# Sums of weight and activation blocks in DRAM, given out group by group instead of in one run, and the additions to the merged blocks put ahead of the last addition to T4

## The chip, the cores and the metric

The kernel runs on one core of a Trainium2 chip. The metric is the device time of one execution in microseconds (us). TensorE (PE) multiplies, VectorE (DVE) and ScalarE (ACT) work on tiles in SBUF, GpSimd (POOL) and SyncE (SP) here mostly issue DMAs. Each engine works through its own queue in order, and waits on semaphores that other engines and DMAs raise.

## The reference, cut to what matters

One layer with a sequence of 1024 and a width of 1024, in float32:

```
h = x @ w_in + b_in            # six blocks of 1024 columns: xa, za, xb, zb, ga, gb
ya = RG_LRU(causal_conv4(xa)) * silu(za)
yb = multi_scale_pool(xb) * silu(zb)
merged = sigmoid(ga) * (ya @ w_proj_a) + sigmoid(gb) * (yb @ w_proj_b)
y = merged @ w_out + b_out
out = layer_norm(2 ** 0.25 * x + y)
```

The two products `ya @ w_proj_a` and `yb @ w_proj_b` are the ones whose operands this change is about.

## The kernel before

Each 1024 x 1024 product is cut into 2 x 2 blocks of 512 and done by Strassen's scheme as Winograd wrote it: seven products of blocks instead of eight, whose operands are sums and differences of blocks. Each product of float32 numbers is three matmuls of a high and a low part (`passes`).

**First stage (to about 530 us).** `x @ w_in` is done in 24 groups of seven products, listed in `order`: first G0, A0, G1, A1 and so on to G7 and A7, then B0 to B7. An A group gives a block of 128 columns of xa and za, a B group of xb and zb, a G group of the gates. A group takes products m1, m7, then what `between()` brings from the groups before (the product m3 of the last group, the gate matmuls `ps_g` of an older A group, the pooling matmuls of an older B group), then m6, m2, m4, m5. ACT copies m1, m7 and m6 out of PSUM (`copied`, line 166; `t7` is the copy of m7). The weights of the next group are loaded by SP into the tiles `ra` and `rb` (lines 109 and 110), split by ACT into high parts (line 85) and by DVE into low parts (line 86), and summed on DVE (lines 124 to 129). Tiles for weights are 14, so SP issues a load only when an older tile is free. The order on PE is written by hand; on ACT and DVE a scheduler sets it, and SP issues in the order of the program.

**Sums in DRAM.** The second stage needs for each of the two products seven operands from the weights (`p1` to `p4` are their sums) and seven from the activations (`t1` to `t4`, from the blocks `ya` and `yb` that the first stage stores). These sums are made by DMA alone: `summed` issues on POOL's queue a plain copy of 1 MB from DRAM to DRAM and then additions (`add_to`, a DMA that adds to its destination, 1 MB too). `weight_sums` has 8 such DMAs for each product (16 in all), `input_sums1` has 5, `input_sums2` has 4. Before the change all are issued where they are called: `input_sums1("a")` and the 16 weight sums stand one behind the other in POOL's queue when the fourth A block's `ya` is stored, at about 228 us, and `input_sums2("b")` with four additions stands in the second stage, where the last blocks of `yb` are stored.

**Second stage, the merge (about 533 to 703 us).** The 14 products of `steps` (a: 1, 2, 6, 5, 3, 7, 4; b: 1, 2, 6, 7, 5, 4, 3) run one after the other on PE, four tiles each (`g`). The raw operands of a step are loaded two steps ahead (`load`), cast one step ahead (`cast`), and SP, ACT and DVE do their parts in the order written. For b the merged block `sums` gets its second term by an addition DMA (`add_to(of(sums, d, h), u)`, the rows `m<-m_b` and `m<-um_b`), and one step later `split_m` on ACT (line 852) and DVE (line 853) splits it, which waits for that DMA. In the loop over `g` a step does `cast(i + 1, g)`, then one `split_m` of the step before, then the copies out of PSUM. `xb4r` is the raw operand T4 of step (b, 4), loaded from `t4b`; `wor` are raw blocks of `w_out` (`load_wo`, `cast_wo`).

**Third stage (703 to 799 us).** `merged @ w_out` (`ps_o`) and the layer norm.

Of the kernel before, what the change touches and what calls it, by code (L numbers as in the profile page):

```python
# [7 lines left out]
F32 = mybir.dt.float32  # L8
# [4 lines left out]
P = 128  # L13
# [3 lines left out]
H = 512  # L17
# [24 lines left out]
def layer_kernel(ctx: ExitStack, tc: tile.TileContext, xq, x, w_in, par, wg, w_pool, wpa, wpb, w_out, rows, out):  # L42
    nc = tc.nc
# [5 lines left out]
    const = pool("const", 1)  # L49
# [231 lines left out]
        nc.sync.dma_start(y_d[n][c], y)  # L281


    def summed(name, *terms):
        t = dram.tile([KQ, P, H], F32, tag=name, name=name)
        nc.gpsimd.dma_start(t, terms[0])
        for u in terms[1:]:
            add_to(t, u)
        return t

    def add_to(t, u):
        nc.gpsimd.dma_start(t, u, accum_op=ALU.add, max_dma_last_dim=2048)

    def weight_sums(n, w):
        a11, a12, a21, a22 = (w[KQ * i:KQ * i + KQ, :, KQ * k:KQ * k + KQ, :].rearrange("n p k m -> n p (k m)")
                              for i in range(2) for k in range(2))
        p1 = summed(f"p1{n}", a21, a22)
        p2 = summed(f"p2{n}", a11, p1)
        src["w", n] = {1: a11, 2: a12, 4: a22, 5: p1, 6: p2, 7: summed(f"p3{n}", a11, a21),
                       3: summed(f"p4{n}", a12, p2)}  # L300


    def input_sums1(n):
# [3 lines left out]

    def input_sums2(n):
        b21, b22 = (y_d[n][KQ:, :, sl] for sl in HALF)
        for j in (6, 7, 4):  # L310
            add_to(src["x", n][j], b22)
        add_to(src["x", n][4], b21)
        src["x", n].update({2: b21, 3: b22})

    src = {}
# [35 lines left out]
    def a_gates(c, xc, xh, xl, sz):  # L351
        gh, gl = gw[c]
        if c + 1 < NK:
            load_g(c + 1)

        r, i = kt(f"r{c}"), kt(f"i{c}")
        for h in range(2):
            pg = [bank(f"ps_g{c}_{h}_{n}") for n in range(2)]
            for k, (w, m) in enumerate(((gh, xh), (gh, xl), (gl, xh))):
                for n in range(2):  # L360
                    nc.tensor.matmul(pg[n], w[HEAD[n], :], m[HEAD[n], HALF[h]], start=k == 0, stop=k == 2)  # L361
            for t, half, ps, s, cb in ((r, LO, pg[0], LO, C_BR), (r, HI, pg[1], HI, C_BR),
                                       (i, LO, pg[0], HI, C_BI), (i, HI, pg[1], LO, C_BI)):
                A.activation(t[half, HALF[h]], ps[s], AF.Sigmoid, bias=par_sb[s, cb + c:cb + c + 1])  # L364

        a = kt(f"a{c}")
        A.activation(a, r, AF.Exp, scale=sc_a[:, c:c + 1])  # L367
        t = r
        A.activation(t, r, AF.Tanh, scale=sc_t[:, c:c + 1])
        V.tensor_tensor(i, i, xc, ALU.mult)  # L370
        V.scalar_tensor_tensor(i, a, 1.0, i, ALU.add, ALU.mult)  # L371
        V.scalar_tensor_tensor(a, a, 1.0, t, ALU.add, ALU.mult)
        V.tensor_scalar(a, a, -1.0, 1.0, ALU.mult, ALU.add)
        A.activation(t, t, AF.Sqrt)
        V.tensor_tensor(i, i, t, ALU.mult)
        hs = t
        V.tensor_tensor_scan(hs, a, i, 0.0, ALU.mult, ALU.add)  # L377
        V.tensor_tensor(hs, hs, sz, ALU.mult)
        A.mul(hs[:, negative(c)], hs[:, negative(c)], -1.0)
        store_y("a", c, hs)  # L380
        if c == KQ - 1:
            input_sums1("a")
            weight_sums("a", wpa)
            weight_sums("b", wpb)
        elif c == NK - 1:
            input_sums2("a")

# [339 lines left out]

    prev_m3 = prev_end = None
    due, last, ends, W = {}, [], [], {}
    for i in range(1, len(order)):  # L730
        kind, c = order[i]
        if i + 1 < len(order):
            W[i + 1] = load_group(i + 1)
        if kind == "B" and c % 2 == 1:
            load_wp(c // 2)
        if i == 1:
            tiles = tiles0
        elif kind == "A":
            tiles, takes = a_outputs(c)
        elif kind == "B":  # L740
            tiles, takes = b_outputs(c)
        else:
            finish, takes = g_outputs(GA if c < 4 else GB, c % 4)
        if i > 1:
            g = Group(f"{kind}{c}", W.pop(i), X, *takes)

        def between():
            for f in due.pop(i, []):
                f()
            if prev_m3:  # L750
                prev_m3()
            if prev_end:
                prev_end()

        if i == 1:
            prev_m3 = None
        elif i >= len(order) - 2:
            g.sums(between)
            prev_m3 = None
            last.append(g)  # L760
        else:
            g.m1()
            g.m7()
            between()
            g.m6()
            g.m2()
            g.m4()
            g.m5()
            if kind == "B" and order[i - 1][0] == "A":
                for f in due.pop(i + 1, []):  # L770
                    f()
            prev_m3 = g.m3
        if kind == "A":
            def prev_end(c=c, tiles=tiles, i=i):
                front = a_front(c, *tiles)
                due.setdefault(i + 2, []).append(lambda: a_gates(c, *front, tiles[1]))
        elif kind == "B":
            def prev_end(c=c, tiles=tiles, i=i):
                for _ in b_front(c, *tiles):
                    pass  # L780
                if c % 2 == 1:
                    due.setdefault(i + 2, []).append(lambda: b_pool(c // 2))
        else:
            prev_end = finish
        if i >= len(order) - 2:
            ends.append((c, *tiles))
            prev_end = None
# [74 lines left out]
    def cast_wo(e, k, raw):  # L862
        hl = wt(f"wo{e}_{k}") if e == 0 else xt(f"wo{e}_{k}")
        split(raw, hl[:, 0, :], hl[:, 1, :])
        wo[e, k] = (hl[:, 0, :], hl[:, 1, :])

    load(0)
    load(1)
    parts6 = [getattr(g, f) for f in ("rest1", "m2", "rest3") for g in last]
# [14 lines left out]
    for i, (n, j) in enumerate(steps):  # L884
        load_sg(i + 1)
        load(i + 2)
        if (n, j) == ("a", 7):
            b_pool(3)
            input_sums2("b")
        if j == 1:  # L890
            a, c, m1, um = [[None] * KQ for _ in range(4)]
        X_, W_ = ([(hi_[:, k, :], lo_[:, k, :]) for hi_, lo_ in ops[i][o:o + 2] for k in range(2)] for o in (0, 2))
        for g in range(KQ):
            if j == 1:
                a[g] = bank(f"pa_{n}{g}")
            elif j == 7:
                c[g] = bank(f"pc_{n}{g}")
            ps = a[g] if j in (1, 6, 5, 3) else c[g] if j != 2 else bank(f"pe_{n}{g}")
            for q in range(KQ):
                sl = slice(q * P, (q + 1) * P)  # L900
                passes(ps, (W_[g][0][:, sl], W_[g][1][:, sl]), X_[q],
                       j in (1, 2, 7) and q == 0, j in (2, 4, 3) and q == KQ - 1)
            cast(i + 1, g)
            if now:
                now.pop(0)()
            if i >= 2:
                next(pieces, None)
            if j == 1:
                m1[g] = et(f"m1_{n}{g}")
                A.copy(m1[g], ps)  # L910
            elif j in KEEP[n]:
                if j == 6:
                    um[g] = wt(f"um_{n}{g}", F32, (P, S)) if n == "a" else kt(f"um_{n}{g}")
                A.copy(um[g][:, HALF[KEEP[n][j]]], ps)
            if (n, j) in DONE:
                d, h = DONE[n, j]
                d += g
                if j == 3:
                    t, u = ps, et(f"c12_{n}{g}") if n == "b" else None
                else:  # L920
                    t = u = m1[g] if j == 2 else um[g][:, HALF[h]]
                    V.tensor_tensor(t, ps, t, ALU.add)
                if n == "a":
                    if d % 2 == 0:
                        sums[d // 2, h] = xt(f"m{d}{h}", F32)
                    V.tensor_tensor(of(sums, d, h), t, sgs[i][g], ALU.mult)
                else:
                    V.tensor_tensor(u, t, sgs[i][g], ALU.mult)
                    if j == 3:
                        V.tensor_tensor(of(sums, d, h), of(sums, d, h), u, ALU.add)  # L930
                        split_m(j, d, h)
                    else:
                        add_to(of(sums, d, h), u)
                        later.append(lambda j=j, d=d, h=h: split_m(j, d, h))
            k = KQ * (i - 9) + g
            if 2 <= k < NK + 2:
                cast_wo(0, k - 2, raws_wo.pop(0))
            if 0 <= k < NK:
                raws_wo.append(load_wo(0, k))
        now, later = later, []  # L940
    merge.close()


# [114 lines left out]
```

## Time and profile before

| | |
|---|---|
| runs | 800.3, 800.05, 797.32 us; median 800.05 |
| profiled execution | 800.89 us, of which the span of the trace is 799.1 |
| PE busy | 759.8 us, 95% of the span |
| DVE, ACT, POOL busy | 74%, 53%, 5% of the span |
| mean granted PE clock | 0.976 of full speed |
| DMA | 139 MB; POOL's queue 38.8 MB, 22.6% of the 16 DMA engines' time |

Busy time is that of an engine between the start and the end of its instructions; a wait shows as idle time ahead of an instruction, with what ended it. The chain of waits is followed back from the last instruction, at each step to what released it. The granted clock is a share of 2.4 GHz: 0.50 is 1.2 GHz. A DMA's row gives its issue; its landing is read from the chain, from the wait that it ended, or from the median of its group.

### The profile page before, as it was taken

What the parts mean: (1) busy time and instruction counts of PE and PEld (TensorE: products, weight loads), DVE (VectorE), ACT (ScalarE), POOL (GpSimd) and SP (SyncE); (2) the same over time, 40 slices, a digit from 0 to 9 for tenths busy, and PEclk for the clock granted to TensorE, in tenths of its full rate; (3) what the DMA queues carried; (4) which work ended last, traced back from release to release, by engine and by line L of the source; (5) the groups of instructions that cost most, each with busy time, mean ns of one, the idle gap of its engine ahead of it and who ended that gap; (6) DMA issues with size and microseconds to landing.
All of it is one profiled execution on the core that took longest, in us unless ns stands there. A gap on an engine that the chain in (4) does not pass through costs nothing.

```text
span 799.1 us, 8834 instructions
## 1 busy us (share of the span) xinstructions
PE 759.8 (95%) x3308; PEld 616.9 (77%) x3308; DVE 589.9 (74%) x764; ACT 423.5 (53%) x543; POOL 40.0 (5%) x67
## 2 busy tenths in 40 slices
PE   8979999999999999896899998999999959999996
PEld 6857788878888888685688887788888848888885
DVE  5997695959586968593967766467988727967587
ACT  5575859595958584956734354234652436430000
POOL 0000000000010100100001001000000020300000
PEclk9999999999999999997999999999999989999999
DMA  8042222222259988795287338568669999656022
GB/s 316 13 161 73 86 82 106 83 106 83 106 155 331 228 218 252 200 221 150 83 167 184 95 121 261 184 222 308 237 227 274 239 263 370 143 146 258 20 87 106
DMA packets 56587, 139.06 MB, mean 174 GB/s; under 512 B 4256, under 2 KB 7456, under 8 KB 56480
## 3 DMA queue, kind: packets, MB, share of 16 engines
q1 hardware_dynamic: 41920, 99.69, 35.0%
q0 software_dynamic: 14624, 38.80, 22.6%
q8 instruction: 26, 0.43, 0.2%
q14 instruction: 17, 0.14, 0.0%
HBM read 114.36 MB, written 56.62 MB: 214 GB/s over the span
## 4 chain that ended last, share of the span: by engine, by line
PE 57%; DVE 18%; issue 9%; ACT 8%; DMA 7%; SPq 1%; POOL 0%; DVEq 0%; ACTq 0%; POOLq 0%
PE ps_o L968 11%; PE a_B L91 7%; PE pa_a L91 5%; PE a_G L91 5%; PE a_A L91 4%; PE pc_b L91 3%; PE c_G L91 3%; PE pa_b L91 3%; PE ps_pool L91 3%; PE c_B L91 2%; PE c_A L91 2%; PE e_B L91 2%; DMA rb_B<-in_w_in 2%; ACT i L364 2%; DVE r L377 1%
## 5 line engine op out<-in xcount | busy, mean ns | idle before, releaser
L968 PE MATMUL ps_o<-wo,m 128*128 128x512 f32 (+1 forms) x408 | 88.5, 379 | 0.0
L968 PEld LDWEIGHTS ps_o<-wo,m 128*128 128x128 f32 x408 | 73.5, 188 | 15.0
L345 DVE SCALAR_TENSOR_TENSOR xc<-xp,par_sb,xc 128x1024 f32<-128x1024 f32 x24 | 30.7, 1281 | 0.3
L852 ACT ACTIVATE m<-m 128x512 fp32r<-128x512 f32 x16 | 9.8, 629 | 39.4 <-DMA m<-m_b 21.0
L125 DVE TENSOR_TENSOR p_G<-p_G,ra_G 128x512 f32<-128x512 f32 x7 | 4.8, 692 | 28.9 <-PE a_G L91 28.9
L91 PE MATMUL pa_a<-oh,oh 128*128 128x512 f32 x64 | 24.9, 389 | 0.0
L91 PE MATMUL pa_a<-ol,oh 128*128 128x512 f32 x64 | 24.9, 389 | 0.0
L91 PE MATMUL pa_a<-oh,ol 128*128 128x512 f32 x64 | 24.9, 389 | 0.0
L91 PE MATMUL pa_b<-oh,oh 128*128 128x512 f32 x64 | 24.9, 389 | 0.0
L91 PE MATMUL pa_b<-ol,oh 128*128 128x512 f32 x64 | 24.9, 389 | 0.0
L91 PE MATMUL pa_b<-oh,ol 128*128 128x512 f32 x64 | 24.9, 389 | 0.0
L364 ACT ACTIVATE r<-ps_g,par_sb 64x512 f32<-64x512 f32 x32 | 21.9, 684 | 3.9 <-PE ps_g L361 3.4
L853 DVE SCALAR_TENSOR_TENSOR m<-m,m 128x512 fp32r<-128x512 f32 x16 | 10.8, 687 | 16.5 <-ACT m L852 16.5
L91 PE MATMUL c_A<-x64h,wd_A 128*128 128x512 f32 x64 | 21.4, 393 | 1.0 <-ACT x64h L594 1.0
L508 DVE SCALAR_TENSOR_TENSOR zb<-ps_pool,par_sb,zb 128x512 f32<-128x512 f32 x16 | 12.0, 749 | 14.0 <-PE ps_pool L91 14.0
L364 ACT ACTIVATE i<-ps_g,par_sb 64x512 f32<-64x512 f32 x32 | 21.9, 684 | 0.5
L91 PE MATMUL pc_b<-oh,oh 128*128 128x512 f32 x32 | 13.6, 424 | 8.7 <-ACT oh L85 8.7
L972 DVE TENSOR_TENSOR z<-ps_o,z 128x512 f32<-128x512 f32 (+1 forms) x17 | 11.1, 657 | 14.1 <-PE ps_o L968 14.0
L91 PE MATMUL c_B<-x64h,wd_B 128*128 128x512 f32 x64 | 21.0, 389 | 0.0
L980 ACT ACTIVATE sd<-mv,eps 128x1 f32<-128x1 f32 x8 | 2.4, 295 | 34.9 <-DVE mv L979 34.9
L371 DVE SCALAR_TENSOR_TENSOR i<-a,i 128x1024 f32<-128x1024 f32 x8 | 9.8, 1226 | 14.9 <-ACT a L367 14.9
L91 PE MATMUL ps_pool<-mixh,wp 128*128 128x512 f32 x64 | 20.7, 394 | 0.0
(447 smaller groups left out, 2401.8 us busy)
## 6 DMA issues: line engine op xcount, KB each, us to landing
sg<-sg SPq DMA_DIRECT2D x16, 512.0 KB, 2.7
ra_A<-in_w_in SPq DMA_DIRECT2D x8, 512.0 KB, 3.4
rb_A<-in_w_in SPq DMA_DIRECT2D x8, 512.0 KB, 3.8
ya<-r SPq DMA_DIRECT2D x8, 512.0 KB, 2.7
ra_B<-in_w_in SPq DMA_DIRECT2D x8, 512.0 KB, 4.0
rb_B<-in_w_in SPq DMA_DIRECT2D x8, 512.0 KB, 7.1
yb<-zb SPq DMA_DIRECT2D x8, 512.0 KB, 3.0
sgla<-sg SPq DMA_DIRECT2D x8, 512.0 KB, 6.1
```

Of the source, the lines that this page charges most:

```text
L91: nc.tensor.matmul(ps, a, b, start=first and i == 0, stop=last and i == 2, skip_group_check=True)
L125: V.tensor_tensor(self.p23[:, 0, :], self.p14[:, 0, :], ra[:, 0, :], ALU.add)
L345: V.scalar_tensor_tensor(xc, xp[:, j:j + S], pcol(C_CONVW, 4 * c + j), xc, ALU.mult, ALU.add)
L364: A.activation(t[half, HALF[h]], ps[s], AF.Sigmoid, bias=par_sb[s, cb + c:cb + c + 1])
L371: V.scalar_tensor_tensor(i, a, 1.0, i, ALU.add, ALU.mult)
L377: V.tensor_tensor_scan(hs, a, i, 0.0, ALU.mult, ALU.add)
L508: V.scalar_tensor_tensor(y[:, HALF[h]], ps, pcol(C_BP, c), y[:, HALF[h]], ALU.add, ALU.mult)
L852: A.mul(of(mh, d, h), of(sums, d, h), sign)
L853: V.scalar_tensor_tensor(of(ml, d, h), of(sums, d, h), sign, of(mh, d, h).bitcast(F32), ALU.mult, ALU.subtract)
L968: nc.tensor.matmul(ps, l, r, start=(k == 0 and i == 0), stop=(k == NK - 1 and i == 2))
L972: nc.vector.tensor_tensor(zt[s][:, lo:hi], ps, zt[s][:, lo:hi], ALU.add)
L980: nc.scalar.activation(sd, mv[:, 1:2], AF.Sqrt, bias=eps)
```

## The change

The DMAs of the sums are no longer issued where they are called. `summed` and `input_sums2` put them into a list, `jobs`, and `run_jobs` issues the first ones of it: two in each G and B group, one in each A group, from the third group on. Ahead of each portion stands a copy of one column of `t7` by ACT into `pace` and a copy of that by POOL, so that POOL reaches the portion when ACT has copied the group's m7. The weight sums are put on the list ahead of the loop, in another order (`p3` ahead of `p2`). In the merge three of the four DMAs of `input_sums2("b")` are issued where all four were, and the fourth, the second addition to T4, behind step (b, 2), whose four additions to `sums` so come ahead of it.

```diff
+    def run_jobs(n, i=None, t=None):
+        if jobs and i is not None:
+            A.copy(pace[:, i:i + 1], t[:, 0:1])
+            nc.gpsimd.tensor_copy(paced[:, i:i + 1], pace[:, i:i + 1])
+        for _ in range(min(n, len(jobs))):
+            jobs.pop(0)()
...
-        nc.gpsimd.dma_start(t, terms[0])
+        jobs.append(lambda: nc.gpsimd.dma_start(t, terms[0]))
         for u in terms[1:]:
-            add_to(t, u)
+            jobs.append(lambda: add_to(t, u))
...
-        for j in (6, 7, 4):
-            add_to(src["x", n][j], b22)
-        add_to(src["x", n][4], b21)
+        for j, u in ((6, b22), (7, b22), (4, b22), (4, b21)):
+            jobs.append(lambda j=j, u=u: add_to(src["x", n][j], u))
...
             input_sums1("a")
-            weight_sums("a", wpa)
-            weight_sums("b", wpb)
...
+    weight_sums("a", wpa)
+    weight_sums("b", wpb)
     for i in range(1, len(order)):
...
+        if i >= 2:
+            run_jobs(1 if kind == "A" else 2, i, g.t7)
...
+    run_jobs(len(jobs))
     load(0)
...
             input_sums2("b")
+            run_jobs(3)
...
         now, later = later, []
+        if (n, j) == ("b", 2):
+            run_jobs(1)
```

The order of instructions on PE, DVE and SP is the same in both programs. On ACT 19 copies of one column are added, each behind or soon behind the copy of m7 of its group. On POOL, where the sums of the weights stand, the queue before is one run of DMAs (`p1b` and so on are the sums, `in_wpb` the weights):

```order
L292 DMA p4a<-p2a 512x512
L286 DMA p1b<-in_wpb 512x512
L292 DMA p1b<-in_wpb 512x512
L286 DMA p2b<-in_wpb 512x512
L292 DMA p2b<-p1b 512x512
L286 DMA p3b<-in_wpb 512x512
L292 DMA p3b<-in_wpb 512x512
```

Now the same DMAs stand in portions, each behind a copy that waits for ACT. L301 is the plain copy, L297 the addition. The rows are those of the groups A3, G4, A4, G5 and A5:

```order
L301 DMA p1b<-in_wpb 512x512
L292 COPY paced<-pace 128x1
L297 DMA p1b<-in_wpb 512x512
L301 DMA p3b<-in_wpb 512x512
L292 COPY paced<-pace 128x1
L297 DMA p3b<-in_wpb 512x512
L292 COPY paced<-pace 128x1
L301 DMA p2b<-in_wpb 512x512
L297 DMA p2b<-p1b 512x512
L292 COPY paced<-pace 128x1
L301 DMA p4b<-in_wpb 512x512
```

So one run became portions: G groups get an addition with a copy behind it, or a copy with the addition that depends on it, or two copies; A groups get one DMA.

In the merge POOL's queue before has both additions to T4 (`t4b`) ahead of the four additions to the merged blocks (`m`, from `m_b`):

```order
L292 DMA t2b<-yb 512x512
L292 DMA t3b<-yb 512x512
L292 DMA t4b<-yb 512x512 x2
L292 DMA m_4149<-m_b_4726 128x512
L292 DMA m_4149<-m_b_4745 128x512
L292 DMA m_4188<-m_b_4764 128x512
L292 DMA m_4188<-m_b_4783 128x512
```

Now the second addition to T4 stands behind the four:

```order
L297 DMA t3b<-yb 512x512
L297 DMA t4b<-yb 512x512
L297 DMA m_4189<-m_b_4765 128x512
L297 DMA m_4189<-m_b_4784 128x512
L297 DMA m_4228<-m_b_4803 128x512
L297 DMA m_4228<-m_b_4822 128x512
L297 DMA t4b<-yb 512x512
L297 DMA m_4594<-um_b_4941 128x512
```

One 1 MB DMA has moved behind four of 256 KB; what follows is as it was.

## Rows read from the trace of the kernel before

**Rows 1.** Timeline of PE where it waited: start, us, instruction, [idle before <-releaser].

```profile
321.75 0.49 PE L361 MATMUL ps_g<-xch,gh 64*128 64x512 f32 x2 [0.62 <-ACT xch L85]
323.81 0.51 PE L361 MATMUL ps_g<-xcl,gh 64*128 64x512 f32 x2 [1.56 <-DVE xcl L86]
...
364.75 0.80 PE L361 MATMUL ps_g<-xch,gh 64*128 64x512 f32 x2 [5.02 <-ACT xch L85]
367.11 0.79 PE L361 MATMUL ps_g<-xcl,gh 64*128 64x512 f32 x2 [1.56 <-DVE xcl L86]
...
398.20 0.50 PE L91 MATMUL a_B<-x13h,wch_B 128*128 128x512 f32 x1 [2.69 <-DVE xbp L441]
...
656.74 0.80 PE L91 MATMUL pc_b<-oh,oh 128*128 128x512 f32 x1 [8.67 <-ACT oh L85]
```

**Rows 2.** Table of stretches: length, PE, PEld, DVE, ACT, POOL busy, PEclk, DMA.

```profile
324.40:327.70 3.30, 3.30 (x12) 2.35 (x10) 1.16 (x3) 3.30 (x5) 0.00 (x0) 0.50 1.07 186
361.90:372.10 10.20, 5.78 (x18) 3.85 (x19) 4.28 (x6) 6.92 (x9) 1.03 (x1) 0.50 0.61 165
399.40:402.80 3.40, 3.40 (x9) 2.65 (x9) 0.52 (x1) 0.10 (x1) 0.00 (x0) 0.50 0.99 176
652.00:662.20 10.20, 5.43 (x12) 3.84 (x13) 7.93 (x10) 8.94 (x14) 0.57 (x1) 0.50 0.95 250
```

**Rows 3.** Chain of waits, first stage: issue, us to landing, DMA.

```profile
230.31 5.72 DMA ra_G<-in_w_in
...
271.45 4.46 DMA ra_G<-in_w_in
...
311.34 8.29 DMA ra_B<-in_w_in
...
355.29 9.85 DMA rb_B<-in_w_in
```

**Rows 4.** Timeline of SP: three issues of loads.

```profile
190.38 0.33 SPq L109 DMA_DIRECT2D ra_G<-in_w_in  x1
...
354.85 0.34 SPq L109 DMA_DIRECT2D ra_B<-in_w_in  x1
...
661.26 6.21 SPq L859 DMA_DIRECT2D wor<-in_w_out  x4
```

**Rows 5.** The tile ra_G: its seven loads.

```profile
DMA to landing us min/median/max: 3.2/3.5/5.7
```

**Rows 6.** Timeline of POOL: five rows of its DMA issues.

```profile
227.75 1.07 POOL L286 DMA_DIRECT2D t1a<-ya  x1 [226.42 <-DMA ya<-r]
...
305.56 1.04 POOL L286 DMA_DIRECT2D p1b<-in_wpb  x1
...
640.86 1.03 POOL L292 DMA_DIRECT2D t4b<-yb  x1 [13.72 <-DMA t4b<-yb]
641.49 3.05 POOL L292 DMA_DIRECT2D m<-m_b  x3
651.71 0.85 POOL L292 DMA_DIRECT2D m<-m_b  x1 [7.18 <-issue]
```

**Rows 7.** Timeline of ACT: a copy of m7, a split of a merged block, a cast.

```profile
305.69 0.57 ACT L166 COPY m_G<-c_G 128x512 f32<-128x512 f32 x1
...
652.68 0.63 ACT L852 ACTIVATE m<-m 128x512 fp32r<-128x512 f32 x1 [21.02 <-DMA m<-m_b]
...
670.00 0.62 ACT L85 CAST wo<-wor 128x512 fp32r<-128x512 f32 x1 [1.40 <-DMA wor<-in_w_out]
```

**Rows 8.** Timeline of DVE in the merge.

```profile
637.95 0.69 DVE L928 TENSOR_TENSOR m_b<-m_b,sglb 128x512 f32<-128x512 f32 x1
...
671.60 1.23 DVE L86 TENSOR_TENSOR ol<-wb5r,oh 128x1024 fp32r<-128x1024 f32 x1 [0.26 <-ACT oh L85]
...
679.69 1.22 DVE L86 TENSOR_TENSOR ol<-wb4r,oh 128x1024 fp32r<-128x1024 f32 x1
```

**Rows 9.** Chain of waits in the merge: one product on PE.

```profile
670.69 10.88 PE pa_b L91 x48
```

More of the change, by code (lines that the diff above doesn't have):

```diff
@@ L281, in store_y, with add_to @@
         nc.sync.dma_start(y_d[n][c], y)
+    jobs = []
+    pace = const.tile([P, 32], F32, name="pace")
+    paced = const.tile([P, 32], F32, name="paced")
+    def run_jobs(n, i=None, t=None):
[4 more added lines that the diff above has]
+            jobs.pop(0)()
+    def add_to(t, u):
+        nc.gpsimd.dma_start(t, u, accum_op=ALU.add, max_dma_last_dim=2048)
     def summed(name, *terms):
         t = dram.tile([KQ, P, H], F32, tag=name, name=name)
-        nc.gpsimd.dma_start(t, terms[0])
+        jobs.append(lambda: nc.gpsimd.dma_start(t, terms[0]))
         for u in terms[1:]:
-            add_to(t, u)
+            jobs.append(lambda: add_to(t, u))
         return t
-    def add_to(t, u):
-        nc.gpsimd.dma_start(t, u, accum_op=ALU.add, max_dma_last_dim=2048)
     def weight_sums(n, w):
@@ L297, in weight_sums @@
         p1 = summed(f"p1{n}", a21, a22)
+        p3 = summed(f"p3{n}", a11, a21)
         p2 = summed(f"p2{n}", a11, p1)
-        src["w", n] = {1: a11, 2: a12, 4: a22, 5: p1, 6: p2, 7: summed(f"p3{n}", a11, a21),
-                       3: summed(f"p4{n}", a12, p2)}
+        src["w", n] = {1: a11, 2: a12, 4: a22, 5: p1, 6: p2, 7: p3, 3: summed(f"p4{n}", a12, p2)}
     def input_sums1(n):
```

## The prediction

> **What bounds the kernel now.** PE is busy for 95% of the span, so the time can fall only where PE waits or runs at half clock. I read first PE's timeline for idle time ahead of an instruction [rows 1]. The places that this change can reach are four: the gate matmuls at 321.75 (0.62 and 1.56 us), the next ones at 364.75 (5.02 and 1.56), a group of products at 398.20 (2.69) and the merge at 656.74 (8.67). Then I read the granted clock around these places [rows 2]: behind each of them stands a stretch at 0.50 of the clock, which is 1.2 GHz. What PE worked in such a stretch took twice its time, so half of it is lost: 1.65, 2.9, 1.7 and 2.7 us. The three places in the first stage so cost 2.18 + 1.65 + 6.58 + 2.9 + 2.69 + 1.7 = 17.7 us, and the one in the merge 8.67 + 2.7 = 11.4 us.
>
> Third, the chain of waits says why. Through the first stage it goes from the load of a group's weights through ACT and DVE to the next such load [rows 3]. The load issued at 230.31 took 5.72 us and the next was issued 41.14 later; that one took 4.46 and the next came 39.89 later; that one took 8.29 and the next [rows 4] came 43.51 later. Take the load off and 35.42, 35.43 and 35.22 us are left: the pair of groups costs ACT and DVE 35.4 us and a load. PE's own pace for a pair is 39.93 (190.38 to 230.31) [rows 3, 4], where nothing waited. So a load may take 4.5 us; each microsecond above that puts ACT and DVE one later against PE. Loads with nothing beside them take 3.2 to 3.5 us [rows 5]. The load at 230.31 had one copy of the sums beside it, issued at 227.75; the one at 311.34 had an addition and a copy, the latter issued at 305.56 [rows 3, 6]. By 311 the lateness was 1.2, and the load of 8.29 made it 5.0; PE then waited 2.18. It so lets 2.8 us of lateness pass without a wait.
>
> In the merge ACT stands for 21 us at the split of a merged block, line 852, until the addition `m<-m_b` has landed [rows 7]. The casts of the next step's operands stand behind it on ACT, and PE waits for those. The addition was ready to go early: DVE wrote the last of the four blocks to be added at 637.95 + 0.69 [rows 8]. But POOL stood until 640.86 for the first addition to T4 to land, issued the second, and then the `m` additions; these landed behind it [rows 6, 7].
>
> **The change, part by part.**
>
> *Sums in portions, first stage.* The 16 weight sums now begin in G1, at some 66 us, and the sums of `ya` come in G6 to A7. No byte is added; what counts is which loads fall beside a sum. A portion starts when ACT has copied m7, in a G group 305.69 + 0.57 [rows 7], and the load that the chain goes through is issued in the same group, 5 us later (311.34) [rows 3]. So in every G group from G2 on that load meets the portion, where before only the loads from 230 on did. In G2, G4 and G6 the portion is an addition with a copy behind it, as at 311: I take 8.29 us, 3.8 above what PE's pace allows. In G3, G5 and G7 it begins with a copy, as at 230: 5.72, so 1.2. Lateness adds up, PE waits for what is above 2.8, and a wait of 2 us or more brings a half-clock stretch (1.7 us lost, by which ACT and DVE catch up): the shortest wait that I read ahead of one is the 2.18. Group by group:
> G2: 3.8 late, PE waits 1.0, 2.8 stay. G3: 4.0 late, waits 1.2, 2.8 stay. G4: 6.6 late, waits 3.8 and 1.7 for the clock, 1.1 stay. G5: 2.3, no wait. G6: 6.1 late, waits 3.3 and 1.7, 1.1 stay. G7: 2.3, no wait. Together 9.3 + 3.4 = 12.7 us.
> In B0 no portion is issued. The load before its gate matmuls (9.85 us with sums beside it [rows 3]) should take some 5 less, near the 3.5 of [rows 5] and a little more, since a second load goes with it. The lateness that it starts with was 5.0 - 2.18 - 1.7 = 1.1 before and is 2.3 now: the wait of 6.58 becomes 6.58 - 5 + 1.2 = 2.8, with 1.7 for the clock. The wait at 398.20 hangs on DVE's work behind these gates; I leave it at 2.69 and 1.7. The stage then loses 12.7 + 2.8 + 1.7 + 4.4 = 21.6 us where it lost 17.7: **3.9 us worse**. Bounds: if a load beside a sum never takes more than the 5.72 of the single copy, each pair is 1.2 later, PE waits 0.8 in G4 and 1.2 in each of G5 to G7 with no half clock, 4.4 in all, and 3.3 + 1.7 in B0, where 2.8 stay: with the 4.4 at 398 the stage loses 13.8, 3.9 better than before. With the 4.46 of the load at 271 nothing is late, B0 waits 6.58 - 5 - 1.1 = 0.5, and it loses 4.9, 12.8 better. If it takes 9.5 beside an addition and 6.5 beside a copy (the 9.85 of [rows 3] is the longest read), the same sum gives waits of 2.2, 0.3, 5.0, 0.3, 5.0 and 0.3 and three half-clock stretches, 18.2 in place of 12.7, and half a microsecond more in B0: 9.9 us worse. I take the middle, since the 8.29 was read at the same place in a group with the same kinds of DMA.
>
> The Trainium skill ("DMA: Bandwidth & Descriptors", section "Queues, rings and completion order") says that each DMA engine goes round between the queues that have work, a packet of each in turn. By it a load beside one busy queue should take about twice its own time, an estimate of 6.8 from that page and [rows 5], beside a copy and beside an addition alike; the 5.72 is below that, the 8.29 and 9.85 are above it, so the rows decide. With 6.8 throughout, the groups' waits and clock come to 11.0 in place of 12.7, and the total to 794.3.
>
> *The pacing copies.* 19 copies of one column on ACT, each under the 0.57 us of a copy of 512 columns [rows 7] and above nothing; on the path once a pair, in a late pair only. By the upper end 3 us, but a column is far nearer to nothing: I take 0 and keep 1 for the range. POOL's copies hold up only the portions, for which nobody waits in this stage. What SP waits for in the merge (`p1b` and the like) is done earlier than before.
>
> *The additions in the merge.* The `m` additions no longer wait for the second addition to T4. Three of them stood in POOL's queue beside a 1 MB addition in flight and the fourth was issued only at 651.71, 10.85 after it [rows 6]; so now three go while the first addition to T4 is in flight and land behind it at about 642, 643 and 644, by the 11 us earlier that the addition ahead of them ends; the fourth follows at about 641 and lands at 645 to 646. ACT then passes line 852 at 642 in place of 652.68, and has the operands ready 4.1 later as before (656.74 - 652.68), at 646.1. PE would be there at 656.74 - 8.67 = 648.07. So the 11.4 us go entirely. What stands behind the moved DMA is new: the second addition to T4 cannot go before the first has landed (640.86) nor before there is room, so about 642, and lands 10.85 later, at 653. `xb4r` reads T4, and SP waits for it with the loads of `wb4r` and the last four `wor` behind it. A `wor` of those was issued at 661.26 and used at 670.00 [rows 4, 7], 8.7 us later; with the loads ahead spread less I take 8 from 653: 661. ACT needs it ahead of its cast of `wb5r`, then 0.6 + 1 us, and DVE then has 9.3 us of work without a gap to the low half of `wb4r` (671.60 to 680.91) [rows 8], so 672. PE, at 10.88 a product [rows 9], would reach step (b, 4) at 669.8: a new wait of **2.1 us**. Bounds: 0, if T4 lands by 650; 6.8 (5.1 and a half-clock stretch) if it lands at 656, as the first one took 13.7 with more loads beside it. The Trainium skill gives a fit for a DMA of POOL's queue (same page, section "Anatomy of one DMA — SWDGE (gpsimd) path"), 2.0 us and the bytes at 436 GB/s, an estimate of 4.4 us for this 1 MB; the rows above show 10.85 and 13.7 for additions from DRAM to DRAM, so they decide; by the fit this wait would be 0 and the total 793.4. Net of the merge 9.3 us better.
>
> **Sum**, against the profiled execution's own 800.9: + 3.9 - 11.4 + 2.1 = 795.5. That execution is 0.8 above the median of the runs, so **795 us**.
>
> **The rivals.**
> 1. *A sum hardly slows a load.* For it: the load at 271.45 took 4.46 beside the end of one sum and the start of another. Against it: 8.29 and 9.85 [rows 3]. With 5.72 the stage gains 3.9 us: 800.9 - 3.9 - 9.3 = 787.7; with 4.46 it is 778.8. I give it **787**, nearer to the first.
> 2. *The loads of the G groups starve* (the other side). With 9.5 beside an addition the stage is 9.9 worse and the gain of the merge is used up: **801.5**; with the late T4 as well (6.8 in place of 2.1) 806. For it: six pairs are now met where three were, and the portion always starts ahead of the load. It decides from about 9.5 us of a load on.
> 3. *A late T4 in the merge*: its second addition lands at 656 or later and SP holds `wor` and `xb4r` back: 800.2 with the first stage as forecast, so **800**. For it: the first one took 13.7 us. Against it: fewer loads are beside the second.
> 4. *The `m` additions don't come earlier*, because POOL finds no room until the first addition to T4 lands (640.86): the first then lands about 5 later, at 646, and PE waits 2 us; the rest stays: 797.5. It changes the sum by 2 us and is in the forecast's own range.
>
> **How the numbers follow.** My forecast (791 to 799, with rival 4) has 0.50, rival 1 0.25, rival 2 0.15, rival 3 0.10. Half a per cent, 4 us, is about what runs of this kernel can tell from no change. Below 796 lie rival 1, three fifths of the forecast and a little of rival 3: 0.58. Above 804 I put 0.13, most of rival 2 (with a late T4 or a longer load still). The rest, 0.29, is within. The range takes in rival 1 at 5.72 and most of rival 2: 785 to 804.
>
> **What the changed profile would show.** For the first stage: the chain of waits through loads of `ra_G` already from 110 us on, 8 us long in G2, G4 and G6; waits of PE at `ps_g` of 1 to 4 us there; one of about 3 us in place of 6.58 at the gates of A7. For the merge: `m` additions issued before 640 and landing near 642; no wait of PE at `pc_b`; ACT waiting some 4 us for `wor` and PE some 2 at the last `pc_b`. What would make it wrong: loads in G groups that stay under 5 us or go over 9, or an ACT that waits for its pacing copy.

## The result, and the profile after

The change takes 800.99 us (median of 14 runs) where the kernel before takes 798.75 (14 runs beside them): a ratio of 1.0032 with an interval of 1.0017 to 1.0047. That is 2.2 us slower, where 5 us faster was forecast; it lies within the half per cent that was called no change, on its far side. The profiled execution took 801.45 us with a span of 799.7, so its trace stands 0.5 above its median; that of before (800.89) stands 2.1 above the 798.75. Sizes below that rest on medians are named so; the traces serve to say where in the program time went.

The page of the changed kernel, its span and the busy times:

```profile
span 799.7 us, 8856 instructions
PE 759.3 (95%) x3308; PEld 615.3 (77%) x3308; DVE 589.7 (74%) x764; ACT 426.5 (53%) x562; POOL 45.1 (6%) x86
```

PE has the same 95% as before. What has changed is where the other 5% lie. The timeline of PE in the changed kernel, at the places that answer to [rows 1] and at a new one (203.66):

```profile
203.66 0.50 PE L372 MATMUL ps_g<-xcl,gh 64*128 64x512 f32 x2 [2.67 <-DVE xcl L86]
...
286.21 0.50 PE L372 MATMUL ps_g<-xcl,gh 64*128 64x512 f32 x2 [0.44 <-DVE xcl L86]
...
326.97 0.49 PE L372 MATMUL ps_g<-xch,gh 64*128 64x512 f32 x2 [0.41 <-ACT xch L85]
...
329.02 0.50 PE L372 MATMUL ps_g<-xcl,gh 64*128 64x512 f32 x2 [1.56 <-DVE xcl L86]
...
366.89 0.79 PE L372 MATMUL ps_g<-xch,gh 64*128 64x512 f32 x2 [2.97 <-ACT xch L85]
...
368.69 0.80 PE L372 MATMUL ps_g<-xcl,gh 64*128 64x512 f32 x2 [1.00 <-DVE xcl L86]
...
399.38 0.50 PE L91 MATMUL a_B<-x13h,wch_B 128*128 128x512 f32 x1 [2.64 <-DVE xbp L450]
...
661.88 0.79 PE L91 MATMUL pc_b<-oh,oh 128*128 128x512 f32 x1 [5.94 <-ACT oh L85]
```

And the table of stretches that answers to [rows 2] (length, busy time of PE, PEld, DVE, ACT, POOL, then the granted clock, DMA share and GB/s):

```profile
206.00:209.00 3.00, 3.00 (x9) 2.33 (x8) 0.00 (x0) 2.94 (x6) 1.18 (x2) 0.50 0.45 175
366.40:372.80 6.40, 4.90 (x16) 3.18 (x17) 3.46 (x6) 4.51 (x7) 0.00 (x0) 0.50 0.00 0
660.00:666.00 6.00, 4.08 (x9) 2.81 (x10) 4.79 (x6) 5.74 (x9) 0.00 (x0) 0.50 1.05 393
```

**The first stage.** A wait of 2.67 us with a stretch at 0.50 of the clock behind it now stands at 203 us, where before PE went through; the wait of 5.02 at the gates of [rows 1] has become 2.97; the one at 398 is as it was. The chain of waits in this stage (issue, us to landing) is that of [rows 3], and begins earlier:

```profile
108.35 7.49 DMA ra_G<-in_w_in
...
191.77 9.92 DMA rb_G<-in_w_in
...
274.31 7.72 DMA ra_G<-in_w_in
...
317.68 7.17 DMA ra_B<-in_w_in
```

When the start of the same products in both traces is compared, the changed kernel is 2.1 us ahead at 65 us, before the first portion (a half-clock stretch lies at another place in the first groups, before any of the moved DMAs). From there it loses 0.8 up to 123, 5.4 up to and behind the gates at 203 and 1.2 up to 288, 7.4 in all; it then loses less than before at the gates of 322 and of 365, 4.1 less. At the gates of 322 the wait is nearly that of [rows 1] (0.41 and 1.56), but the clock from 325 to 335 is granted in full, where [rows 2] have a stretch at 0.50. At 399 it is 1.2 behind: **3.3 us lost** in the stage up to there. Between the same two products the traces of `m_only`, `m_no4`, `m_late` and `half5` below, whose first stage is that of before, lie between 0.5 faster and 0.4 slower than the trace of before, so 3.3 is clear of what such a reading varies by. Another 1.2 goes at 487, where PE waits for DVE's `zb` (3.5 us, 2.3 before); that wait is 1.9 in `w_only`, which has the same portions, so it is not put down to them.

**The merge.** The additions to the merged blocks do come earlier. The timeline of POOL in the changed kernel, to hold against [rows 6]:

```profile
629.25 1.02 POOL L297 DMA_DIRECT2D t4b<-yb  x1 [12.98 <-issue]
633.45 0.88 POOL L297 DMA_DIRECT2D m<-m_b  x1 [3.19 <-DVE m_b L943]
...
643.47 0.85 POOL L297 DMA_DIRECT2D m<-m_b  x1 [3.67 <-issue]
645.51 1.03 POOL L297 DMA_DIRECT2D t4b<-yb  x1 [1.19 <-issue]
```

The four are issued from 633.45 to 643.47. The first three go within 0.7 us of the end of DVE's work on their blocks, while the first addition to T4 is in flight. The fourth block was written at 641.04, but its addition was issued at 643.47, 0.3 us after that addition to T4 had landed (issued at 629.25, 13.92 us). The timeline of ACT in the changed kernel, from the first split of a merged block, to hold against [rows 7]:

```profile
645.23 0.63 ACT L865 ACTIVATE m<-m 128x512 fp32r<-128x512 f32 x1 [11.15 <-DMA m<-m_b]
...
649.87 0.57 ACT L929 COPY um_b<-pa_b 128x512 f32<-128x512 f32 x1
660.26 0.62 ACT L85 CAST wo<-wor 128x512 fp32r<-128x512 f32 x1 [9.83 <-DMA wor<-in_w_out]
660.79 1.04 ACT L85 CAST oh<-wb7r 128x1024 fp32r<-128x1024 f32 x1
```

ACT passes the first split at 645.23, 7.5 us earlier than in [rows 7]. Seven instructions on, after 649.87, it stands again, 9.83 us, now at the first cast of a block of `w_out`. The second half of `wb7r`, which PE wants at its 661.88, is cast behind that. So the wait of 21.02 us in [rows 7] was cut to 11.15, and 9.83 of it came back at the next DMA in ACT's order. PE is 8.8 us earlier at the head of step (b, 7), relative to 620 us, and loses most of it inside the step. At the last product the merge has given **1.8 us** in this trace, not 9.3.

Why was that block of `w_out` late? The timeline of SP in the changed kernel:

```profile
632.18 5.87 SPq L822 DMA_DIRECT2D wb5r<-p1b  x2
645.26 6.47 SPq L872 DMA_DIRECT2D wor<-in_w_out  x4
```

Its load was issued at 645.26, as soon as the first `m` addition had landed (in the kernel before it waits for the same), and landed when ACT went on, at 660.26: 15 us. Ahead of it in SP's queue stood the operands of step (b, 5), issued from 631 on. The tile `wb5r` of the changed kernel:

```profile
DMA to landing us min/median/max: 24.9/25.8/26.7
```

The same tile in the kernel before:

```profile
DMA to landing us min/median/max: 15.8/16.5/17.2
```

These two loads now run beside four `m` additions and the second addition to T4, issued at 645.51 in the middle of them, and take 9 us longer. The chain of waits in the merge of the changed kernel goes through an `m` addition and then through a later block of `w_out` in the same queue. The same block took 3.19 us in the kernel before:

```profile
638.95 10.36 DMA m<-m_b
...
649.36 12.25 DMA wor<-in_w_out
```

### The profile page after: what moved, and what is told of

It is laid out like the page before. It is cut to its first block, busy times and chain, and to the rows that moved or that the text cites. A ratio compares the mean times of both kernels' runs of the same rounds, so it can differ in the third digit from the quotient of the medians.

```text
span 799.7 us, 8856 instructions
## 1 busy us (share of the span) xinstructions
PE 759.3 (95%) x3308; PEld 615.3 (77%) x3308; DVE 589.7 (74%) x764; ACT 426.5 (53%) x562; POOL 45.1 (6%) x86
## 4 chain that ended last, share of the span: by engine, by line
PE 58%; DVE 19%; DMA 10%; ACT 8%; issue 4%; SPq 1%; DVEq 0%; ACTq 0%; POOLq 0%
PE ps_o L985 11%; PE a_B L91 8%; PE pa_a L91 5%; PE a_G L91 5%; PE a_A L91 4%; PE pa_b L91 3%; PE pc_a L91 3%; PE c_B L91 3%; PE ps_pool L91 3%; PE c_G L91 3%; DMA wor<-in_w_out 2%; PE e_B L91 2%; PE c_A L91 2%; DMA ra_G<-in_w_in 2%; ACT i L375 2%
## 5 line engine op out<-in xcount | busy, mean ns | idle before, releaser
L292 POOL COPY paced<-pace 128x1 f32<-128x1 f32 x19 | 6.2, 329 | 359.9 <-ACT pace L291 359.9
L91 PE MATMUL pa_b<-oh,oh 128*128 128x512 f32 x64 | 24.9, 389 | 0.0
L91 PE MATMUL pa_a<-oh,ol 128*128 128x512 f32 x64 | 24.9, 389 | 0.0
L91 PE MATMUL pa_b<-ol,oh 128*128 128x512 f32 x64 | 24.9, 389 | 0.0
L91 PE MATMUL pa_a<-oh,oh 128*128 128x512 f32 x64 | 24.9, 389 | 0.0
L91 PE MATMUL pa_a<-ol,oh 128*128 128x512 f32 x64 | 24.9, 389 | 0.0
L85 ACT CAST wah_G<-ra_G 128x1024 fp32r<-128x1024 f32 x7 | 7.4, 1052 | 30.6 <-DMA ra_G<-in_w_in 30.6
L381 DVE TENSOR_TENSOR i<-i,xc 128x1024 f32<-128x1024 f32 x8 | 9.8, 1224 | 18.8 <-ACT i L375 18.8
L86 DVE TENSOR_TENSOR wo<-wor,wo 128x512 fp32r<-128x512 f32 x16 | 10.8, 688 | 16.5 <-ACT wo L85 16.5
L989 DVE TENSOR_TENSOR z<-ps_o,z 128x512 f32<-128x512 f32 (+1 forms) x17 | 11.1, 656 | 13.8 <-PE ps_o L985 13.7
L91 PE MATMUL ps_pool<-mixh,wp 128*128 128x512 f32 x64 | 20.9, 395 | 0.0
```

The costliest lines, as they stand in the source:

```text
L85: A.copy(hi, raw)
L86: V.tensor_tensor(lo, raw, hi.bitcast(F32), ALU.subtract)
L91: nc.tensor.matmul(ps, a, b, start=first and i == 0, stop=last and i == 2, skip_group_check=True)
L292: nc.gpsimd.tensor_copy(paced[:, i:i + 1], pace[:, i:i + 1])
L989: nc.vector.tensor_tensor(zt[s][:, lo:hi], ps, zt[s][:, lo:hi], ALU.add)
```

## The experiments

The theory after this result: (1) the portions cost about 4 us in the first stage, because they fall beside the loads of G groups; (2) the move in the merge frees ACT from the `m` additions, but the DMAs that then run at the same time hold back the loads in SP's queue, and ACT stands at a `w_out` block in place of the split. The rival to (1): the portions cost nothing, and what was lost is noise of the first groups or of the merge. The rival to (2): the T4 addition has no part in it, or `w_out` is late whatever the sums do. The first four kernels below ran beside 17 runs of the kernel before (median 797.8), the last three beside 11 (798.75); each has 4 to 12 runs of its own.

**The portions alone (w_only).** The changed kernel, with all four additions of `input_sums2("b")` issued together again:

```diff
-            run_jobs(3)
+            run_jobs(4)
...
-        if (n, j) == ("b", 2):
-            run_jobs(1)
```

> The portions in the first stage as in the change, the merge as before (all four additions to t2b, t3b and t4b in one place). Theory: the loads of ra_G now fall beside an addition in G2, G4 and G6, ACT and DVE come later against PE, and PE waits at the gates; by the trace of the change the first stage is some 3 to 4.5 us longer and the merge has its wait of 8.7 us as before: 802 to 803.5 beside 798.75, a ratio of 1.004 to 1.006. Rival: the portions cost nothing and the loss of the change is in the merge: within 1 us of before.

Measured: 803.03 us against 797.8, a ratio of 1.0065 (1.0044 to 1.0086). The portions alone cost 5.2 us (3.5 to 6.9). The tile `ra_G` of this kernel, to hold against [rows 5]:

```profile
DMA to landing us min/median/max: 3.2/6.1/8.4
```

The median load went from 3.5 to 6.1 us. So the portions do cost time; that it is by these loads is shown by `a3` below. The trace says where only roughly. Against that of before, which is itself 3.1 above the 797.8, it loses 3.1 us from 65 to 397, gets 1.6 back behind the wait of 2.65 that ends at 400.68, where the clock stays at 1.00 and the kernel before has a stretch at 0.50 ([rows 2]), and loses 1.6 in the merge, whose DMAs stand in the order of before. Whether that last part comes from the portions or is chance isn't shown.

**The move alone (m_only).** The kernel before, with only the second addition to T4 moved:

```diff
-        add_to(src["x", n][4], b21)
+        if n == "a":
+            add_to(src["x", n][4], b21)
...
         now, later = later, []
+        if (n, j) == ("b", 2):
+            add_to(src["x", n][4], y_d[n][KQ:, :, HALF[0]])
```

> The sums in one run as before, only the second addition to T4 moved behind step (b, 2). Theory: the m additions land 11 us earlier, but the moved addition runs beside the loads of wb5r and wor, ACT waits for wor, and PE gets back some 2 of the 11.4 us: 796 to 798, a ratio of 0.996 to 0.999. Rival 1, the move is worth its full 9 us and the portions eat it: 790, 0.989. Rival 2, the move itself loses: over 800, 1.002 or more.

Measured: 796.13 us against 797.8, 0.9982 (0.9968 to 0.9997): the move gives 1.7 us, with an interval of 0.2 to 2.6. With the portions' 5.2 the sum is 3.5, and the whole change was measured at 2.2, with an interval of 1.4 to 3.8: the two parts add up. ACT in this kernel shows the same exchange:

```profile
639.44 0.63 ACT L853 ACTIVATE m<-m 128x512 fp32r<-128x512 f32 x1 [10.38 <-DMA m<-m_b]
...
654.92 0.62 ACT L85 CAST wo<-wor 128x512 fp32r<-128x512 f32 x1 [10.28 <-DMA wor<-in_w_out]
```

As the first stage is that of before, the portions have no part in the wait for `w_out`.

**The move, without the moved DMA (m_no4).** As `m_only`, but the second addition to T4 is not made at all.

```diff
-        if (n, j) == ("b", 2):
-            add_to(src["x", n][4], y_d[n][KQ:, :, HALF[0]])
```

> As the kernel with the move alone, but the second addition to T4 is left out (T4 lacks one block, so one operand of the last products is not the reference's). Theory: it is this 1 MB addition that holds up the loads of step 5 and of wor; without it ACT waits only for the m additions at about 642 and PE has no wait of over 1 us in the merge: 787 to 790, a ratio of 0.985 to 0.989. Rival: the m additions themselves beside the loads do it, or the wor loads that stand behind them in SP's queue: 795 or more, with ACT still waiting for wor.

Measured: 792.04 us, 0.9931 (0.991 to 0.9951), 5.8 us faster than before and 4.1 faster than `m_only`. ACT in this kernel:

```profile
640.31 0.63 ACT L853 ACTIVATE m<-m 128x512 fp32r<-128x512 f32 x1 [9.81 <-DMA m<-m_b]
...
650.87 0.62 ACT L85 CAST wo<-wor 128x512 fp32r<-128x512 f32 x1 [5.37 <-DMA wor<-in_w_out]
```

The wait for `w_out` falls from 10.28 to 5.37, not to nothing, and the time stays above the 787 to 790 that were expected. So the second addition to T4 is about half of the cause. `wb5r` takes 20.3 to 21.2 us here, less than the 25.5 to 27.4 of `m_only`, more than the 15.8 to 17.2 of before.

The landings show where the other half comes from. From the issue of the first load of `wb7r` to the landing of the second of `wb5r`, behind which the `w_out` blocks stand in SP's queue, it takes 20.0 us in the kernel before (20.5 in `w_only`, 20.9 in `a3`, which have the old order), 24.8 in `m_no4` and 30.3 in `m_only`. The first addition to T4 is in flight beside these loads in all of them. So the early `m` additions hold the queue back by some 4 to 5 us and the second addition to T4 by 5.5 more. In `m_no4` the first addition to T4 lands at 638.15 and the last `m` addition at 646.36; what lies between has `m` additions alone beside SP's loads. The DMA queues there, from 639 to 645, with POOL's as q0 and SP's as q1 (packets, MB, time of the packets as a share of 16 engines' time; it can pass 100%, as packets overlap):

```profile
q0 software_dynamic: 411, 0.76, 68.2%
q1 hardware_dynamic: 433, 0.84, 41.5%
```

And from 646.4 to 650.8, with no addition left:

```profile
q1 hardware_dynamic: 934, 1.75, 105.1%
```

SP's queue moves 0.14 MB a microsecond beside additions and 0.40 alone. Both queues get through about as many packets, but a packet of an addition takes about 1.7 times the time of a packet of a load (68.2% for 411, 41.5% for 433).

**No sums in G groups (a3).** As `w_only`, with the same DMAs given out three to an A group, two to a B group and none to a G group:

```diff
-        if i >= 2:
-            run_jobs(1 if kind == "A" else 2, i, g.t7)
+        if i >= 2 and kind != "G":
+            run_jobs({"A": 3, "G": 0, "B": 2}[kind], i, g.t7)
```

> The portions alone (merge as before), but three DMAs in each A group and none in a G group, so that no addition is in flight when ra_G is loaded. Theory: it is these loads alone that make PE wait; they land in under 4.5 us again, PE waits nowhere at the gates of A0 to A5, and the first stage is 4 us or more shorter than with the portions of the change and no longer than before: 793 to 798, a ratio of 0.993 to 0.999. Rival: any sum in flight anywhere costs the same, by the loads of ra_A and the stores that it slows: as with the portions of the change, 802 to 803.5.

Measured: 790.88 us, 0.9912 (0.9895 to 0.993): 12.2 us faster than `w_only` and 6.9 faster than before, more than was expected. The same 16 weight sums, the same bytes, the same number to a pair of groups; the group in which they are issued differs, and there are 12 pacing copies in place of 19 (0.19 us of ACT each, so 1.3 us at most of the 12.2). The tile `ra_G` of this kernel:

```profile
DMA to landing us min/median/max: 3.2/3.3/4.1
```

The loads of the chain now land after 3.2 to 3.4 us, as loads with nothing beside them did (the 4.1 is the first of the seven, ahead of any sum). It is the loads of the A groups that are slowed now: those of `ra_A` take 7.5 us by the median, where they took 3.4 before, and PE waits for none of them. Of the waits of PE at the gates 0.86 and 1.29 us are left, where [rows 1] add up to 8.8. The merge is that of before, and PE's longest wait by engine and line (us, times, longest) is there:

```profile
PE pc_b L91 <- ACT oh L85: 9.4, 1, 9.4
```

**`w_out` out of ACT's way (m_late).** As `m_only`, with each block of `w_out` cast two tiles later:

```diff
-            if 2 <= k < NK + 2:
-                cast_wo(0, k - 2, raws_wo.pop(0))
+            if 4 <= k < NK + 4:
+                cast_wo(0, k - 4, raws_wo.pop(0))
```

> The move alone, and the casts of the w_out blocks (cast_wo) two tiles later in the order on ACT and DVE: the first behind the first tile of step (b, 7) instead of behind the third of (b, 6). Theory: with the move alone ACT stands 10 us at the first cast_wo, because that block's load lies in SP's queue behind the operands of step 5, and PE waits 5.6 us for the cast of wb7r that is queued behind it. With the casts later PE does not wait inside (b, 7); what is left is a wait of 1 to 3 us at the start of step (b, 5) or (b, 4): 791 to 794.5 beside 796.1 of the move alone, a ratio to before of 0.991 to 0.996. Rival: PE waits for the operands of step 5 themselves, whose loads land late too; the wait only goes to (b, 5), and the time stays at 796, 0.998.

Measured: 792.39 us against 798.75, 0.9933 (0.9912 to 0.9954), 6.4 us faster. PE has no wait in (b, 7) any more: the cast was indeed what held up `wb7r`. But the next of the late loads shows one step on:

```profile
PE pa_b L91 <- ACT oh L85: 3.1, 1, 3.1
```

That is the head of (b, 5), whose `wb5r` takes 25.7 to 26.3 us here. So the order on ACT only decides which late load PE meets first; the lateness of SP's queue stays.

**The bytes earlier (half5).** The kernel before, with the order in POOL's queue as it was, but the four additions of `input_sums2("b")` cut in two: the half for the blocks of `yb` stored first goes at the start of step (a, 5), the other at (a, 7).

```diff
-    def input_sums2(n):
+    def input_sums2(n, rows=slice(0, KQ)):
...
-            add_to(src["x", n][j], b22)
-        add_to(src["x", n][4], b21)
+            add_to(src["x", n][j][rows], b22[rows])
+        add_to(src["x", n][4][rows], b21[rows])
...
+        if (n, j) == ("a", 5):
+            input_sums2("b", slice(0, 2))
         if (n, j) == ("a", 7):
             b_pool(3)
-            input_sums2("b")
+            input_sums2("b", slice(2, KQ))
```

> The kernel before, with the four additions of input_sums2 for b cut in two: the part for the blocks 4 and 5 of yb, stored long before, goes at the start of step (a, 5), the part for the blocks 6 and 7 where all stood. Theory: it is the 4 MB of additions between 598 and 653 us that fill the DMA engines and hold up the merge; with half of them gone from there the m additions and the loads land in time, and the merge loses its 11.4 us: 786 to 790, a ratio of 0.985 to 0.990. Rival: the DMA engines are as full at 555 to 580, and the additions only move the wait there: 795 or more.

Measured: 788.25 us, 0.9873 (0.9848 to 0.9897), 10.5 us faster. ACT in this kernel:

```profile
639.01 0.63 ACT L852 ACTIVATE m<-m 128x512 fp32r<-128x512 f32 x1 [7.03 <-DMA m<-m_b]
...
658.80 0.62 ACT L85 CAST wo<-wor 128x512 fp32r<-128x512 f32 x1 [1.63 <-DMA wor<-in_w_out]
```

The first halves were issued from 515.89 on, 0.6 us after the store of their blocks had landed. The `m` additions still stand behind both additions to T4 in POOL's queue, but of those only halves of 512 KB are left at this point, and the second of them landed at 626.50, ahead of the first `m` addition (issued at 631.40). `wb5r` lands in 14.0 to 14.8 us, ACT finds the first four blocks of `w_out` there when it comes to them, and the fifth comes 1.63 late (1.40 in [rows 7]). PE has no wait from 625 us to the end of the merge.

**Both (a3half5).** `a3` and `half5` in one kernel.

```diff
-        if i >= 2:
-            run_jobs(1 if kind == "A" else 2, i, g.t7)
+        if i >= 2 and kind != "G":
+            run_jobs({"A": 3, "G": 0, "B": 2}[kind], i, g.t7)
...
+        if (n, j) == ("a", 5):
+            input_sums2("b", slice(0, 2))
+            run_jobs(4)
         if (n, j) == ("a", 7):
             b_pool(3)
-            input_sums2("b")
-            run_jobs(3)
+            input_sums2("b", slice(2, KQ))
+            run_jobs(4)
```

> Both cures together: portions of three DMAs in A groups only, and the additions for b cut in two, the first part at step (a, 5). Theory: the two act in different stages and add up: 6.9 us of the first and what the second gives alone: 780 to 784, a ratio of 0.978 to 0.983. Rival: the one takes from the other, not below 787.

Measured: 779.18 us, 0.9758 (0.9736 to 0.978). It beats the kernel before by 19.6 us and the changed one by more. That is a little more than the 6.9 and 10.5 of the two alone, and below the 780 to 784 that were expected; the table below has a likely reason, since `a3` alone lost time in a merge that `half5` mends. ACT in this kernel:

```profile
626.76 0.64 ACT L865 ACTIVATE m<-m 128x512 fp32r<-128x512 f32 x1 [6.96 <-DMA m<-m_b]
...
645.58 0.62 ACT L85 CAST wo<-wor 128x512 fp32r<-128x512 f32 x1 [0.59 <-DMA wor<-in_w_out]
```

The gain of the merge can be read clear of the first stage in each trace, as the shift of PE's start on the same matmuls against the kernel before, at the last matmul of (b, 3) less that at 620 us, ahead of the merge's wait:

| kernel | at 620 us | at the last matmul | the merge gave |
|---|---|---|---|
| changed kernel | +2.4 | +0.6 | 1.8 |
| m_only | -2.6 | -4.8 | 2.1 |
| m_late | -4.0 | -9.0 | 5.0 |
| m_no4 | -1.2 | -8.8 | 7.6 |
| half5 | +0.3 | -11.4 | 11.7 |
| a3half5 | -11.9 | -23.6 | 11.7 |
| w_only | +0.7 | +2.3 | -1.6 |
| a3 | -10.8 | -9.7 | -1.2 |

Each row is one trace against one. The last two have the merge of before and should show 0, so a figure of this column is good to about 1.5 us.

## Why the prediction was wrong

**The step that failed: the merge.** The prediction had ACT pass line 852 at 642 "and has the operands ready 4.1 later as before", and "So the 11.4 us go entirely". The first half came about: ACT passed at 645.23 in a trace that is 2.4 later at this place. The second half took over an interval from the kernel before, in which the `m` addition was the last thing to land: what stood between the split and the cast of `wb7r` cost nothing there. One of those instructions is the first `cast_wo`, whose load is issued only when the first `m` addition has landed. Before, SP's queue was empty by then (the second load of `wb5r` landed at 646.86), so the load took 4.5 us (issued at 652.71, landed at 657.19), and ACT came to its cast at 657.58. In the changed kernel the loads ahead of it were still on their way, and it took 15. The prediction put nothing for this load. The merge gave 1.8 us by the trace and 1.7 by the median of `m_only`, in place of 9.3; the size of the stall itself was right, as `half5` and `a3half5` both take 11.7 out of the merge, beside the 11.4.

**Rival 3 named the right addition and the wrong way of holding loads back.** It had SP hold back `wor` and T4's load behind a late addition, for the last four `wor` and step (b, 4). The second addition landed late, as it said from 656 on: it took 13.8 us from 645.51, to 659.33, against the 10.85 on which the forecast rested. That 10.85 is the time to POOL's next issue; the addition landed after 10.54, and the first one, put at 13.7, after 14.29. (The Trainium skill's fit for POOL's queue, "DMA: Bandwidth & Descriptors", section "Anatomy of one DMA — SWDGE (gpsimd) path", gives an estimate of 4.4 us; the trace does not agree.) But the wait fell on the first four `wor` and on `wb5r`, a step and a half earlier, because the loads that are held back are those in SP's queue while the addition runs (`wb5r` in 25.5 to 27.4 us with it and in 20.3 to 21.2 without), not only those that read its result. At (b, 4) PE waited 0.72 us where 2.1 was put. The prediction asked of the moved DMA who waits for its result. It didn't ask which loads run beside it, nor beside the `m` additions once these go earlier. Rival 3's 800 and rival 2's 801.5 lie next to the measured 800.99; as neither's mechanism is what happened, that is luck.

**The first stage: right in kind and in sum, its terms less so.** 3.9 us worse was forecast; `w_only` gives 5.2 (3.5 to 6.9), the trace 3.3. Loads of 8.29 beside an addition were put in G2, G4 and G6; they took 7.49, 7.03 (9.92 for the second of the pair) and 7.72. Beside a copy 5.72 was put in G3, G5 and G7; they took 4.24, 3.53 and 7.17. So four groups are hit, not six: the 5.5 us put in G4 came about (5.4), of the 5.0 put in G6 only 1.2 did. The loss up to 288 is 7.4 us where 12.7 was put up to G7. The gain behind it, against the losses of before, is smaller too: 4.1 where 8.8 was put (12.7 less 3.9). The two errors cancel. In B0 2.8 with a half-clock stretch was forecast at the gates, and 2.97 and 1.00 came with one; 398 stayed at 2.64. That a wait of 2 us or more brings a half-clock stretch, as the sum took it, is not so each time: the wait of 2.65 in `w_only` brought none (1.00 from 402 to 406), that of 2.67 in `m_late` neither (1.00 from 398 to 402), where the 2.69 of before did.

**The pacing copies** cost nothing that shows: each takes ACT 0.19 us, only POOL's copies wait for them, and none of the waits of PE in the changed kernel leads to them.

**Rivals 1, 2 and 4.** Rival 1 (loads hardly slowed) falls by the loads above. Rival 2 (9.5 beside every addition) falls too: of the loads of the chain one got there, the 9.92 above. (Its chance doesn't fit its figure: 0.13 stands above 804 as most of rival 2, whose own 801.5 lies below.) Rival 4 falls for three of the four `m` additions, which were issued as soon as DVE had written their blocks. The fourth did wait for the first addition to T4 to land, some 2.4 us; ACT's wait was for the first.

What stays open: the shares of the `m` additions and of the second addition to T4 (4 to 5 and 5.5 us of SP's queue) are read from one trace each. No run took the `m` additions or the first addition to T4 away.

## What to carry to other kernels

A wait that ends last hides every wait behind it on the same engine: before a long wait is priced as gone, list each instruction between it and the next consumer with the DMA that it needs, and price those loads beside what will then be in flight. Place large DRAM-to-DRAM transfers by the loads that they run beside, not only by how many go to a group: here the same sums cost 5 us in the groups whose loads the chain goes through and gave 7 in the other groups. When bytes must be moved before a deadline, starting half of them as soon as their data exists did more here (10.5 us) than letting a shorter transfer pass them in the queue (1.7 us).

## What was not expected of the hardware

A load that meets a 1 MB addition from DRAM to DRAM is not slowed by a fixed share. In the first stage `ra_G`, which takes 3.2 to 3.5 us alone, took 7.0 to 7.7 beside an addition, and `rb_G`, the second of its pair (4.1 to 4.5 alone), 9.2 to 9.9. An addition doesn't weigh at once: a load of `ra_G` issued 0.1 us ahead of one (71.34 and 71.43) still took 3.25, its `rb_G`, issued 1.2 us behind the addition, 11.25. Two loads that stood in SP's queue through two additions to T4 and four `m` additions took 24.9 and 26.7 us.

An addition is slowed by its company as well. The second one to T4 took 10.5 us in the kernel before (10.6 in `w_only`, 10.7 in `a3`), where SP's queue was soon empty, and 13.7 to 13.8 in the changed kernel, `m_only` and `m_late`, where loads ran beside it to its end.

A 1 MB addition behind another one, or a fourth `m` addition beside a 1 MB one, was issued each time 0.3 us behind a landing, with no wait that the profile names: behind the landings at 612.24, 625.81 and 651.40 in the kernel before, at 643.16 and 645.21 in the changed one. Three `m` additions beside a 1 MB addition went at once. That looks like a limit to what POOL's queue holds; no run here tests it.
